# Attention and recurrence of one denoising step, in a fixed order of TensorE

## Chip, cores and metric

The kernel runs on one core of a Trainium2 chip. The metric is the device time of one execution in microseconds (us); smaller is better. Weights and inputs lie in HBM in float32, and so do the outputs.

## What is computed

Two layers of a hybrid network run over 1152 tokens: 1024 latent tokens and 128 context tokens. Each layer projects its input once, gives the columns to three groups of heads, projects their outputs back, and ends with a SwiGLU feed-forward part. The change touches two of the three groups. Cut to that, the reference is:

```python
def _mla_attend(q_nope, q_rope, k_nope, k_rope, v):          # 8 heads, 96 score rows, 64 value columns
    ...
        s = jnp.einsum('bqhd,bkhd->bhqk', qn_i, k_nope) + jnp.einsum('bqhr,bkr->bhqk', qr_i, k_rope)
        prob = jax.nn.softmax(s.astype(F32) * MLA_SCALE, axis=-1).astype(v.dtype)
        return jnp.einsum('bhqk,bkhd->bqhd', prob, v)
...
    def step(S, inp):                                        # RWKV-7: 2 directions, 4 heads of 64
        r_t, w_t, k_t, v_t, kk_t, a_t = inp
        s_kk = jnp.einsum('dbhvk,dbhk->dbhv', S, -kk_t)
        S = S * w_t[..., None, :] + s_kk[..., :, None] * (kk_t * a_t)[..., None, :] + v_t[..., :, None] * k_t[..., None, :]
        return S, jnp.einsum('dbhvk,dbhk->dbhv', S, r_t)
...
    y = out[0] + out[1][:, ::-1]
    mu = jnp.mean(y, -1, keepdims=True)
    var = jnp.mean(jnp.square(y - mu), -1, keepdims=True)
    y = ((y - mu) * lax.rsqrt(var + RW_GN_EPS)).reshape(B, T, RW_W) * p['rw_gn_g'] + p['rw_gn_b']
```

## The kernel before

Nearly all time goes to products of float32 operands. A precise product takes three TensorE instructions (`mm3`, L119 to L121): each operand is split into a high and a low part, and high x high, high x low and low x high are summed in PSUM. Products named f32 in the recurrence are float32 matmuls, which the profile counts as two instructions each.

A layer has a stage in which **attention** (`mla`) and the **recurrence** (`rwkv`) run together. In layer 0 it lies at 369 to 996 us of the profile, in layer 1 at 2319 to 2986 us. Before it stand projections, after it the output projection `w_out` and the feed-forward part.

*Attention.* A unit is one head and 512 latent queries; every second unit also takes the 128 context queries. There are 16 units a layer. For each of a unit's 9 key blocks of 128, `attend` issues a score triple (L119 to L121, 512 columns), an Exp on ScalarE (L767, tile `P`), and two value products (L772), and GpSimd sums the P tiles into `acc` (L774). The softmax needs row maxima: they are found two units ahead by coarse scores (L733, reduced by VectorE at L738 and L744), turned by an identity (`eye`, L751) into row 96 of the query tile `qT`. `load` clears that row by a GpSimd memset (L726) and loads the other 96 from `qd` in DRAM. `mla` is a generator; it yields after three key blocks.

*Recurrence.* The tokens go in 9 segments of 128 (one of context, eight latent), each of 2 chunks of 64, all heads and both directions at once. For a segment `rw_prep` makes the chunk matrices M1 (L965: a tile of 64 rows, upper half first, then lower half, one PSUM bank each) and the transposes BT (L972). `rw_solve` inverts 16x16 diagonal blocks, 14 rows on VectorE (L999, L1000), with the blocks going out to DRAM and back (`ltd`, `Db`, `xbd`, `xz`). `rw_double` (L1022 to L1041) grows the inverses to 64x64. `rw_scan` takes the chunks in order: R, then UV (L1065), then the change of the state UV x BT (L1071) and the outputs, UV x M1 (L1075) and state x AR (L1077), eight of each. `rw_post` (L1119 to L1145) does the group norm, with ScalarE's Sqrt and VectorE's reciprocal (L1129), the bonus and the gate. `rwkv` prepares segments three ahead and calls `next(other)` between these parts to let attention go on.

*What sets the order.* The program is written in that order, but a scheduler sorts each engine's instructions by its own estimates of when operands are ready. On TensorE it interleaves instruction by instruction what stands near in the program. `streams` gives each kind of work its PSUM banks: scores "012", value products "3", prep and post "4", doubling "5", scan "67".

TensorE can be used as one tile of 128x128 or as smaller ones. Scores are 128*128, value products 128*64, L965 and L972 64*128, L1071 and L1075 128*64 in the profile's naming, L1077 and L1065 64*64, the doubling 64*64 and 32*32. Below, a **group** is a run of consecutive matmuls of one tile shape in TensorE's order, a **change** the step from one group to the next.

## Time and profile before

| | |
|---|---|
| runs | 3965.17, 3952.76, 3957.21 us |
| median | 3957.21 us |
| span of the profiled execution | 3970.9 us |
| TensorE busy in it | 3842.4 us (97%) |
| VectorE / ScalarE / GpSimd busy | 2006.7 / 1096.0 / 1311.2 us |
| stage of layer 0 / layer 1 | 627 / 667 us |
| the rest | 2677 us |

The profiled execution is one run of its own; its span is all of its time that the profile gives. PE is TensorE's matmuls, DVE VectorE, ACT ScalarE, POOL GpSimd, SP the engine that issues most DMAs. PEclk is the clock that TensorE was granted, as a share of full speed. Instructions overlap on TensorE, and the ends of matmuls are modelled: what a group costs is read from the start of its first instruction to the start of the next group's, not from busy time.

### The profile page before, as it was taken

The page shows a single profiled execution, that of the slowest core. Times are in us where ns is not written, and L with a number is a line of the kernel's source. Part 1 is how long each engine was busy: PE and PEld are TensorE (multiplying, and loading weights), DVE is VectorE, ACT ScalarE, POOL GpSimd, SP SyncE. Part 2 cuts the span into 40 slices and gives each one's busy share as a digit, 9 for nine tenths or more (in the row PEclk, how much of TensorE's full clock was granted, in tenths as well). Part 3 has the DMA queues.
Part 4 walks back from the last instruction along what each step waited for, and adds up shares of the span by engine and source line. Part 5 has one row for each costly group of instructions (what it writes and reads, how often), then busy time and mean ns, then how long its engine had stood idle before and what let it go on. Part 6 is the DMA issues. An engine that isn't in the chain of part 4 may idle for free. (4 is left out here: it accounts for less than half of the span.)

```text
span 3970.9 us, 61645 instructions
## 1 busy us (share of the span) xinstructions
PE 3842.4 (97%) x25091; PEld 3178.9 (80%) x25091; DVE 2006.7 (51%) x3428; ACT 1096.0 (28%) x2066; POOL 1311.2 (33%) x1221
## 2 busy tenths in 40 slices
PE   8999999998999999999999989999998999999996
PEld 6887666665988888988888966666658999999995
DVE  3556776645643333343555557644457633333346
ACT  3452333234321111111244423321343321111111
POOL 2324544335411111112541445432354311111145
PEclk9998899998999999999999978886899999999998
DMA  7476443213332222122336554331223211111122
GB/s 284 152 225 159 108 98 86 57 48 115 111 118 91 75 85 78 61 64 75 102 122 181 155 126 111 75 83 33 61 91 126 96 43 43 40 39 40 42 89 76
DMA packets 463452, 383.60 MB, mean 97 GB/s; under 512 B 171020, under 2 KB 397192, under 8 KB 461952
## 3 DMA queue, kind: packets, MB, share of 16 engines
q1 hardware_dynamic: 388864, 271.67, 24.7%
q10 hardware_dynamic: 68480, 92.34, 7.0%
q0 software_dynamic: 5824, 15.66, 1.3%
q8 instruction: 197, 3.23, 0.3%
q14 instruction: 87, 0.71, 0.1%
HBM read 277.74 MB, written 101.84 MB: 96 GB/s over the span
## 5 line engine op out<-in xcount | busy, mean ns | idle before, releaser
L121 PE MATMUL b<-hyh,w 128*128 128x384 f32 x2544 | 858.0, 337 | 0.0
L119 PE MATMUL b<-hyh,w 128*128 128x384 f32 x2448 | 822.4, 336 | 0.0
L120 PE MATMUL b<-hyl,w 128*128 128x384 f32 x2448 | 821.3, 335 | 0.0
L316 POOL TENSOR_TENSOR w<-wr,w 128x2048 fp32r<-128x2048 f32 x64 | 297.1, 4642 | 1190.4 <-ACT w L313 987.6
L121 PEld LDWEIGHTS b<-hyh,w 128*128 128x128 f32 x2544 | 478.7, 188 | 24.5 <-issue 23.9
L119 PEld LDWEIGHTS b<-hyh,w 128*128 128x128 f32 x2448 | 459.6, 188 | 20.8 <-issue 19.4
L120 PEld LDWEIGHTS b<-hyl,w 128*128 128x128 f32 x2448 | 459.5, 188 | 9.7 <-issue 8.3
L774 POOL TENSOR_TENSOR acc<-acc,P 128x512 f32<-128x512 f32 x256 | 338.9, 1324 | 375.5 <-ACT P L767 349.6
L1274 DVE TENSOR_TENSOR fs<-fs,b 128x384 f32<-128x384 f32 x132 | 72.9, 553 | 631.2 <-PE b L121 625.6
L313 ACT CAST w<-wr 128x2048 fp32r<-128x2048 f32 (+2 forms) x86 | 161.2, 1874 | 580.7 <-PE b L120 516.4
L120 PE MATMUL b<-w,hidh 128*128 128x512 f32 x756 | 299.5, 396 | 0.0
L121 PE MATMUL b<-w,hidl 128*128 128x512 f32 x756 | 299.4, 396 | 0.0
L119 PE MATMUL b<-w,hidh 128*128 128x512 f32 x756 | 298.3, 396 | 0.0
L126 DVE TENSOR_TENSOR hidl<-fs,hidh 128x384 fp32r<-128x384 f32 x126 | 233.0, 1851 | 81.3 <-ACT hidh L125 79.2
L1288 DVE TENSOR_TENSOR acc<-acc,b 128x512 f32<-128x512 f32 x288 | 191.4, 684 | 139.0 <-PE b L121 139.0
L767 ACT ACTIVATE P<-b 128x512 f32<-128x512 f32 x256 | 148.8, 595 | 363.4 <-PE b L121 324.9
L738 DVE TENSOR_REDUCE mx<-b 128x1 f32<-128x512 f32 x256 | 172.1, 682 | 135.8 <-PE b L733 134.4
L772 PE MATMUL b<-P,vt 128*64 128x256 f32 x1024 | 192.7, 447 | 14.0 <-ACT P L767 13.8
L119 PE MATMUL b<-w,hyh 128*128 128x256 f32 x576 | 167.3, 292 | 9.9 <-issue 3.2
L125 ACT CAST hidh<-fs 128x384 fp32r<-128x384 f32 x126 | 64.4, 512 | 397.3 <-DVE fs L1274 397.3
L119 PEld LDWEIGHTS b<-w,hidh 128*128 128x128 f32 x756 | 142.1, 188 | 35.1 <-issue 1.7
L121 PEld LDWEIGHTS b<-w,hidl 128*128 128x128 f32 x756 | 142.1, 188 | 34.3
(433 smaller groups left out, 7481.0 us busy)
## 6 DMA issues: line engine op xcount, KB each, us to landing
wr<-in_ffn_w_in_dram SPq DMA_DIRECT2D x88, 512.0 KB, 4.7
fx<-in_ada_w_dram SPq DMA_DIRECT2D x28, 1024.0 KB, 5.1
wr<-in_ffn_w_out_dram SPq DMA_DIRECT2D x22, 1024.0 KB, 4.9
wr<-in_ada_w_dram SPq DMA_DIRECT2D x20, 1024.0 KB, 9.1
zin<-zd SPq DMA_DIRECT2D x36, 384.0 KB, 4.2
xres<-x ACTq DMA_DIRECT2D x27, 512.0 KB, 3.6
wr<-in_w_in_dram SPq DMA_DIRECT2D x12, 1024.0 KB, 6.1
qT<-qd SPq DMA_DIRECT2D x32, 384.0 KB, 6.4
```

The lines of the kernel that those rows point to most:

```text
L119: mm(out, ah, bh, start=(i == 0), stop=False)
L120: mm(out, ah, bl, start=False, stop=False)
L121: mm(out, al, bh, start=False, stop=(i == n - 1))
L126: (lo_eng or self.nc.vector).tensor_tensor(lo, src, hi.bitcast(F32), op=ALU.subtract)
L313: self.nc.scalar.copy(hi, r)
L316: (eng or self.nc.gpsimd).tensor_tensor(lo[:, s], r[:, s], hi[:, s].bitcast(F32), op=ALU.subtract)
L738: nc.vector.tensor_reduce(mx[:, i, c:c + 1], p, axis=AX.X, op=ALU.max)
L767: nc.scalar.activation(P[:, 0:nq], p[:, 0:nq], AF.Exp, scale=MLA_SCALE)
L772: nc.tensor.matmul(po[64 * i:64 * i + 64, 0:w], vt[:, kt_], P[:, w * i:w * i + w], start=(n == 0), stop=(kt_ == kts[-1]))
L774: nc.gpsimd.tensor_tensor(acc[:, 0:nq], acc[:, 0:nq], P[:, 0:nq], op=ALU.add)
L1274: nc.vector.tensor_tensor(s, s, u[:, 0:BLK], op=ALU.mult)
L1288: nc.vector.tensor_tensor(acc[i][:, w], acc[i][:, w], p, op=ALU.add)
```

## The change

Only the stage changes; the code outside it stays as it is.

*Attention* goes in batches of key blocks: [0,1], [2,3], [4,5], [6,7], [9], the context's block with the last. A batch issues its score triples and one or two steps for the maxima of the unit two ahead; its value products are issued one batch later (`before`). The generator yields twice a batch: behind the scores and behind the value products. Row 96 of `qT` comes with the load from `qd`, which got a row of zeros in `fill`.

*Recurrence* goes in slots. A slot lets attention issue a batch's scores, does its `first` work, three rows of a running solve, lets attention issue value products, and does its other work. `rw_prep`, `rw_solve`, `rw_double`, `rw_scan` and `rw_post` became generators that yield behind whole groups of matmuls. There are 69 slots a layer: 10 ahead of the first scan, 6 for each of 9 segments, 5 behind. `RW_PACE` gives attention an extra batch now and then. Segments are prepared two ahead.

*Order.* From `mla` to the end of attention TensorE's instructions stay in the order of the program (`manual_schedule`); the other engines are sorted as before.

*Groups.* `rw_prep` alternates between the two halves of rows, with a PSUM bank for each. `rw_scan` issues all of UV x BT, then all of UV x M1, then all of state x AR, into one bank. `rw_post` takes the root of four numbers a token on GpSimd, and two matmuls by the identity spread them.

Attention and its helper steps:

```diff
+RW_PACE = 1.08
...
+        self.qd = d([8, 97, 2, T], "qd")
...
+        for h in range(8):
+            nc.scalar.dma_start(self.qd[h, 96].rearrange("x t -> (x t)").rearrange("(p n) -> p n", p=128), o[:, 0:18])
...
-            nc.gpsimd.memset(t[96:97, 0].bitcast(F32), 0.0)
-            nc.sync.dma_start(t[0:96].bitcast(F32), self.qd[h, :, :, q0:q0 + nq])
+            nc.sync.dma_start(t[0:97].bitcast(F32), self.qd[h, :, :, q0:q0 + nq])
...
-        def attend(h, q0, kT, vt, qT, steps, slots):
...
+        def scores(kT, qT, kt_, nq, P):
+            ks = slice(128 * kt_, 128 * kt_ + 128)
+            p = self.psum("as")
+            self.mm3(p[:, 0:nq], [(kT[0][:, ks], kT[1][:, ks], qT[0], qT[1])])
+            nc.scalar.activation(P[:, 0:nq], p[:, 0:nq], AF.Exp, scale=MLA_SCALE)
+        def finish(h, q0, nq, po, acc):
...
-                P = self.t(ap, [128, 512], "P", bufs=3) if n else acc
-                p = self.psum("as")
...
-                slots[0] -= 1
-                for _ in range(-(-len(steps) // (slots[0] + 1))):
-                    steps.pop(0)()
-                for i in parts:
-                    nc.tensor.matmul(po[64 * i:64 * i + 64, 0:w], vt[:, kt_], P[:, w * i:w * i + w], start=(n == 0), stop=(kt_ == kts[-1]))
...
-                if n % 3 == 2 and n < 8:
-                    yield
...
-            yield
+            steps = [carry, *prepare(n + 2)[1:]]
...
+            for g, kts in enumerate(([0, 1], [2, 3], [4, 5], [6, 7], [9])):
+                todo = steps[g] if g < len(steps) else []
+                for k in kts:
+                    P = Ps[k] = self.t(ap, [128, 512], "P", bufs=4)
+                    scores(kT, qT, k, 512, P)
+                    if k:
+                        nc.gpsimd.tensor_tensor(acc, Ps[0] if k == 1 else acc, P, op=ALU.add)
...
+                yield
+                if before:
+                    before()
+                def products(h=h, q0=q0, vt=vt, acc=acc, po=po, Ps=Ps, kts=kts, ctx=ctx):
+                    if not po:
+                        po.append(self.psum("po"))
+                    for k in kts:
+                        for i in range(2):
+                            nc.tensor.matmul(po[0][64 * i:64 * i + 64, 0:256], vt[:, k], Ps[k][:, 256 * i:256 * i + 256], start=(k == 0), stop=(k == 9))
...
+                before = products
...
+                yield
+            carry = steps[5] if len(steps) > 5 else []
```

The slots of `rwkv`:

```diff
+        def solved(i):
+            while i in solves:
+                row()
+        pace = [0.0]
+        def slot(*work, first=()):
+            pace[0] += RW_PACE - 1
+            if pace[0] >= 1:
+                pace[0] -= 1
+                next(other, None)
-        for n in range(len(segs) + ahead):
-            if n < len(segs):
-                ready[n] = self.rw_prep(segs[n], rp, hv)
-                attend(2 if n < ahead else 1)
-                xz[n] = self.rw_solve(rp, ready[n][3], self.xbd[n % 4])
-            i = n - ahead
...
-            if i >= 0:
-                self.rw_double(rp, ready[i][3], xz[i], Q)
...
+            next(other, None)
+            for f, *a in first:
+                f(*a)
+            for _ in range(3):
+                row()
+            next(other, None)
+            for f, *a in work:
+                f(*a)
...
+        next(other)
+        start(0)
+        slot((go, prep, 0))
+        slot((go, prep, 0), (solve, 0), (start, 1))
+        slot((go, prep, 0))
+        slot((go, prep, 1))
+        slot((go, prep, 1), (solve, 1))
+        slot((go, prep, 1))
+        slot((solved, 0), (go, double, 0))
+        for _ in range(3):
+            slot((go, double, 0))
+        for i in range(n):
+            scan = self.rw_scan(segs[i], rp, Y, state, xz[i], *ready[i])
+            j = i + 2
+            def turn():
+                next(scan, None)
...
+            def posting():
+                for p in posts:
+                    next(p, None)
+            slot((turn,), (start, j))
+            slot((turn,), (go, prep, j), first=[(posting,)])
+            slot((turn,), (go, prep, j), (solve, j), first=[(solved, i + 1), (go, double, i + 1), (posting,)])
+            slot((turn,), (go, prep, j), first=[(go, double, i + 1), (posting,)])
+            slot((turn,), first=[(go, double, i + 1), (posting,)])
+            slot((turn,), first=[(go, double, i + 1), (posting,)])
...
+            ready.pop(i), xz.pop(i)
+        posts = [self.rw_post(l, b, rp, Y, g2, brk) for b in post]
+        for _ in range(5):
+            slot(*((next, p, None) for p in posts))
```

`rw_prep`, `rw_solve` and `rw_double`:

```diff
+        M1 = self.t(rp, [128, 2, 4, 2, 128], "M1", bufs=3)
+        BT = self.t(rp, [128, 2, 4, 2, 64], "BT", bufs=3)
...
+        yield AR, EP, UV, M1, BT
...
-        for h in range(2):
-            for j in range(2):
-                p = self.psum("ra").rearrange("p (c t) -> p c t", t=128)
-                for ct in range(2):
-                    for u in range(2):
-                        nc.tensor.matmul(p[:, 2 * ct + u], BK[u][rows[h], 2 * j + ct, bks[h]], AR[u][rows[h], 2 * j + ct], start=True, stop=True)
...
+                    for h in range(2):
+                        nc.tensor.matmul(ps[h][:, 2 * ct + u], BK[u][rows[h], 2 * j + ct, bks[h]], AR[u][rows[h], 2 * j + ct], start=True, stop=True)
...
+            yield
+        ps = [self.psum("ra") for _ in range(2)]
+        for cj in range(4):
+            for u in range(2):
+                for h in range(2):
-                    nc.tensor.transpose(p[:, o:o + 64], BK[u][rows[h], cj, bks[h]], self.ident[rows[h], rows[h]])
-            nc.scalar.copy(BT[:, h].rearrange("p c u k -> p (c u k)"), p)
-        return AR, EP, UV, M1, BT
+                    nc.tensor.transpose(ps[h][:, o:o + 64], BK[u][rows[h], cj, bks[h]], self.ident[rows[h], rows[h]])
...
-        return xz
+        yield xz
...
-            return self.psum("rb")[:, 0:256].rearrange("p (j b t) -> p j b t", b=2, t=16)
+            return self.psum("ra")[:, 0:256].rearrange("p (j b t) -> p j b t", b=2, t=16)
```

`rw_scan`, `rw_post` and `run`:

```diff
+            p = self.psum("rc")
+            ps_, po = (p[:, a:a + 256].rearrange("p (c u t) -> p c u t", c=2, u=2) for a in (0, 256))
...
-                cj = 2 * j + ct
-                nc.tensor.matmul(po[rg, ct, u], UV[:, h, u, cj, :], M1[:, h, cj, u, 64:128], start=True, stop=(S is None))
-                if S is not None:
-                    nc.tensor.matmul(po[rg, ct, u], S[rg, ct, u, :], AR[u][rg, cj, 64:128], start=False, stop=True)
+                nc.tensor.matmul(ps_[rg, ct, u], BT[:, h, 2 * j + ct, u, :], UV[:, h, u, 2 * j + ct, :], start=True, stop=True, skip_group_check=True)
+            for n, (h, ct, u, rg) in enumerate(gu):
+                nc.tensor.matmul(po[rg, ct, u], UV[:, h, u, 2 * j + ct, :], M1[:, h, 2 * j + ct, u, 64:128], start=(n < 2 or S is None), stop=(S is None), skip_group_check=True)
+            if S is not None:
+                for h, ct, u, rg in gu:
+                    nc.tensor.matmul(po[rg, ct, u], S[rg, ct, u, :], AR[u][rg, 2 * j + ct, 64:128], start=False, stop=True, skip_group_check=True)
...
-    def rw_post(self, l, blocks, rp, Y, g2, brk):
...
+    def rw_post(self, l, b, rp, Y, g2, brk):
...
+        yield
+        p = self.psum("ra")
+        for ct in range(2):
+            nc.tensor.matmul(p[:, 2 * ct:2 * ct + 2], sq[:, ct], self.bones[:, 0:128:64], start=True, stop=True)
+        q = self.t(rp, [128, 4], "po_q", bufs=2)
+        nc.vector.tensor_scalar(q, p[:, 0:4], 1.0 / 64, 64e-5, op0=ALU.mult, op1=ALU.add)
+        self.rsqrt(q, q, 4)
+        wide = tmp("po_t")
+        nc.gpsimd.tensor_copy(wide.rearrange("p c (h o) -> p (c h) o", o=64), q.rearrange("p (c o) -> p c o", o=1).to_broadcast([128, 4, 64]))
...
-        nc.tensor.matmul(p, self.bones, sq, start=True, stop=True)
-        s = tmp("po_t")
-        nc.vector.tensor_scalar(s, p, 1.0 / 64, 64e-5, op0=ALU.mult, op1=ALU.add)
-        nc.scalar.activation(s, s, AF.Sqrt)
-        nc.vector.reciprocal(s, s)
-        nc.gpsimd.tensor_tensor(yc, yc, s, op=ALU.mult)
...
+            nc.tensor.matmul(p[:, ct], wide[:, ct], self.ident, start=True, stop=True)
+        nc.vector.tensor_tensor(yc, yc, p, op=ALU.mult)
...
-            self.streams(**{"as": "012", "po": "3", "ra": "4", "rb": "5", "rc": "67"})
+            self.streams(**{"as": "0127", "po": "3", "ra": "45", "rc": "6"})
...
+            order = ExitStack()
+            order.enter_context(self.tc.manual_schedule(engines={mybir.EngineType.PE}))
...
+            order.close()
```

The order of TensorE shows what this does. In the names, `b` is a PSUM bank, `xz` the inverses, `S` the state, the numbers tell tiles apart; line numbers of the changed kernel are its own (scores L120 to L122, coarse scores L736, `eye` L754, value products L861, L1061 for L965, L1070 for L972, L1178, L1181 and L1184 for L1071, L1075 and L1077).

TensorE at the outputs of a chunk, layer 0, before (`M` is M1, `UV` and `S` as above):

```order
L1071 MATMUL b_1347_7284<-UV_5125,BT_5127 64x64
L1075 MATMUL b_1348_7293<-M_912_5126,UV_5125 64x64
L1077 MATMUL b_1348_7293<-AR_919_5144,S_6786 64x64
L1075 MATMUL b_1348_7293<-M_912_5126,UV_5125 64x64
L1077 MATMUL b_1348_7293<-AR_919_5144,S_6786 64x64
L1075 MATMUL b_1348_7293<-M_912_5126,UV_5125 64x64
L1077 MATMUL b_1348_7293<-AR_927_5171,S_6786 64x64
L1075 MATMUL b_1348_7293<-M_912_5126,UV_5125 64x64
L1077 MATMUL b_1348_7293<-AR_927_5171,S_6786 64x64
L1075 MATMUL b_1348_7293<-M_912_5126,UV_5125 64x64
L1077 MATMUL b_1348_7293<-AR_919_5144,S_6786 64x64
L772 MATMUL b_1331_7207<-P_7222,vt_6383 64x256 x2
```

TensorE at the same place in the changed kernel:

```order
L1178 MATMUL b_1089_6141<-UV_4496,BT_4498 64x64 x8
L1181 MATMUL b_1089_6141<-M_758_4497,UV_4496 64x64 x8
L1184 MATMUL b_1089_6141<-AR_765_4515,S_5874 64x64 x2
L1184 MATMUL b_1089_6141<-AR_773_4542,S_5874 64x64 x2
L1184 MATMUL b_1089_6141<-AR_765_4515,S_5874 64x64 x2
L1184 MATMUL b_1089_6141<-AR_773_4542,S_5874 64x64 x2
L120 MATMUL b_1096_6179<-qT_550_3683,kT_556_3689 128x512
L121 MATMUL b_1096_6179<-qT_550_3683,kT_556_3689 128x512
L122 MATMUL b_1096_6179<-qT_550_3683,kT_556_3689 128x512
```

Eight products of UV and M1 now stand together, and then eight of the state, where the two alternated one by one.

TensorE at scores among the doubling of the recurrence, layer 0, before:

```order
L972 MATMUL b_1286_6959<-cst_63,BK_1279_6915 128x64
L1022 MATMUL b_1421_7620<-xz_5902,M_1028_5705 64x32 x5
L119 MATMUL b_1337_7223<-qT_578_3777,kT_581_3780 128x512
L120 MATMUL b_1337_7223<-qT_578_3777,kT_581_3780 128x512
L121 MATMUL b_1337_7223<-qT_578_3777,kT_581_3780 128x512
L1022 MATMUL b_1421_7620<-xz_5902,M_1028_5705 64x32 x6
L772 MATMUL b_1331_7207<-acc_7208,vt_6383 64x256 x2
L1071 MATMUL b_1347_7284<-UV_5125,BT_5127 64x64 x7
L733 MATMUL b_1334_7214<-kT_582_3781,qT_577_3776 128x512
L733 MATMUL b_1335_7217<-kT_582_3781,qT_577_3776 128x512
```

The same place of TensorE in the changed kernel:

```order
L120 MATMUL b_1066_6017<-qT_552_3685,kT_555_3688 128x512
L121 MATMUL b_1066_6017<-qT_552_3685,kT_555_3688 128x512
L122 MATMUL b_1066_6017<-qT_552_3685,kT_555_3688 128x512
L736 MATMUL b_1067_6023<-kT_556_3689,qT_551_3684 128x512
L120 MATMUL b_1069_6027<-qT_552_3685,kT_555_3688 128x512
L121 MATMUL b_1069_6027<-qT_552_3685,kT_555_3688 128x512
L122 MATMUL b_1069_6027<-qT_552_3685,kT_555_3688 128x512
L736 MATMUL b_1070_6033<-kT_556_3689,qT_551_3684 128x512
L754 MATMUL b_1071_6036<-eye_3679 97x128
L1136 MATMUL b_1072_6039<-xz_5741,M_873_5069 32x32 x16
L861 MATMUL b_1040_5844<-P_5892,vt_4442 64x256 x2
L861 MATMUL b_1040_5844<-P_5902,vt_4442 64x256 x2
```

A score triple stood alone between pieces of the doubling; now two triples with their coarse scores stand together, and the doubling and the value products of the batch before follow as wholes.

TensorE at the transposes in `rw_prep`, layer 0, before, all in one bank (BK's half of rows is the same in all eight):

```order
L1022 MATMUL b_1421_7620<-xz_5902,M_1028_5705 64x32
L972 MATMUL b_1286_6959<-cst_63,BK_1271_6888 128x64
L972 MATMUL b_1286_6959<-cst_63,BK_1279_6915 128x64
L972 MATMUL b_1286_6959<-cst_63,BK_1271_6888 128x64
L972 MATMUL b_1286_6959<-cst_63,BK_1279_6915 128x64
L972 MATMUL b_1286_6959<-cst_63,BK_1271_6888 128x64
```

The same place of TensorE in the changed kernel:

```order
L1163 MATMUL b_1061_5977<-S_5874,AR_773_4542 64x64
L1070 MATMUL b_1063_5996<-cst_63,BK_1002_5677 128x64
L1070 MATMUL b_1064_5997<-cst_63,BK_1002_5677 128x64
L1070 MATMUL b_1063_5996<-cst_63,BK_1010_5704 128x64
L1070 MATMUL b_1064_5997<-cst_63,BK_1010_5704 128x64
L1070 MATMUL b_1063_5996<-cst_63,BK_1002_5677 128x64
```

Neighbours now lie in different banks and in different halves of the rows.

## Rows read from the trace of the kernel before

**Rows 1.** Page, the span in 40 slices, tenths: VectorE and the clock granted.

```profile
DVE  3556776645643333343555557644457633333346
PEclk9998899998999999999999978886899999999998
```

**Rows 2.** Windows: length, busy time (instructions) of each engine, clock, DMA share, GB/s.

```profile
369.00:996.00 627.00, 601.38 (x5241) 400.13 (x5242) 397.11 (x788) 211.84 (x425) 282.95 (x333) 0.90 0.37 90
2319.00:2986.00 667.00, 644.79 (x5202) 422.41 (x5201) 386.77 (x777) 209.31 (x419) 275.04 (x319) 0.83 0.33 80
500.00:900.00 400.00, 395.50 (x3979) 266.49 (x3979) 246.43 (x507) 127.06 (x258) 160.33 (x186) 0.95 0.32 72
```

**Rows 3.** Timeline of TensorE, layer 0: start, length, engine, line, operation, tile.

```profile
554.93 0.68 PE L1065 MATMUL b<-R,xz 64*64 64x64 f32 x16
555.55 0.65 PE L772 MATMUL b<-P,vt 128*64 128x256 f32 x4
556.13 0.50 PE L733 MATMUL b<-kT,qT 128*128 128x512 f32 x1
...
932.70 1.08 PE L772 MATMUL b<-P,vt 128*64 128x256 f32 x8
933.71 0.50 PE L119 MATMUL b<-qT,kT 128*128 128x512 f32 x1
```

**Rows 4.** The same timeline, score triples and row halves of the preparation.

```profile
424.77 1.16 PE L965 MATMUL b<-AR,BK 64*128 64x128 f32 x8
425.86 0.50 PE L119 MATMUL b<-qT,kT 128*128 128x512 f32 x1
...
427.45 0.44 PE L772 MATMUL b<-P,vt 128*64 128x256 f32 x2
...
611.87 0.50 PE L119 MATMUL b<-qT,kT 128*128 128x512 f32 x1
...
612.76 0.24 PE L1028 MATMUL b<-xz,Q 64*64 64x32 f32 x1
```

**Rows 5.** The same timeline, outputs of a chunk.

```profile
614.16 0.69 PE L1071 MATMUL b<-UV,BT 128*64 128x64 f32 x16
614.67 0.28 PE L1075 MATMUL b<-M,UV 128*64 128x64 f32 x2
...
615.39 0.33 PE L1077 MATMUL b<-AR,S 64*64 64x64 f32 x2
```

**Rows 6.** Timeline of TensorE, layer 1, transposes of the preparation.

```profile
2502.85 0.71 PE L972 MATMUL b<-cst,BK 64*128 64x64 f32 x8
2503.49 0.30 PE L751 MATMUL b<-eye 128*97 128x128 f32 x1
```

**Rows 7.** Groups of VectorE, 369 to 996 us: count, busy, mean ns, idle before, releaser.

```profile
L738 DVE TENSOR_REDUCE mx<-b 128x1 f32<-128x512 f32 x128 | 85.8, 683 | 54.2 <-PE b L733 53.4
L999 DVE TENSOR_TENSOR pr_x<-Xb,Db 64x4 f32<-64x4 f32 (+6 forms) x126 | 68.4, 543 | 2.6
...
L1000 DVE TENSOR_REDUCE Xb<-pr_x 64x2 f32<-64x4 f32 (+6 forms) x126 | 29.2, 232 | 2.5
...
L126 DVE TENSOR_TENSOR hyl<-wr,hyh 128x384 fp32r<-128x384 f32 (+1 forms) x23 | 17.1, 799 | 4.8 <-ACT hyh L125 4.8
L1129 DVE RECIPROCAL po_t<-po_t 128x256 f32<-128x256 f32 x9 | 15.7, 1748 | 4.7 <-ACT po_t L1128 4.7
```

**Rows 8.** DMA issues of the program: count, KB each, median us to landing.

```profile
xz<-xbd SPq DMA_DIRECT2D x72, 128.0 KB, 3.2
...
ltd<-M SPq DMA_DIRECT2D x36, 128.0 KB, 2.6
...
xbd<-Xb SPq DMA_DIRECT2D x36, 64.0 KB, 2.6
...
Db<-ltd SPq DMA_DIRECT2D x18, 64.0 KB, 2.6
```

**Rows 9.** Windows as in Rows 2, two stretches of like work in the two layers.

```profile
700.00:762.00 62.00, 62.00 (x607) 40.85 (x607) 38.13 (x89) 14.13 (x31) 22.44 (x25) 0.92 0.17 36
2700.00:2763.00 63.00, 63.00 (x374) 41.27 (x372) 21.22 (x51) 9.61 (x21) 12.80 (x17) 0.51 0.15 31
```

More of the change, by code (lines that the diff above doesn't have):

```diff
@@ new lines, in rwkv, with start, go, solve @@
+        ready, xz, prep, double, post = {}, {}, {}, {}, []
+        def start(i):
+            if i < n:
+                prep[i] = self.rw_prep(segs[i], rp, hv)
+                ready[i] = next(prep[i])
+        def go(stream, i):
+            if i in stream:
+                next(stream[i], None)
+        solves = {}
+        def solve(i):
+            if i < n:
+                solves[i] = self.rw_solve(rp, ready[i][3], self.xbd[i % 4])
+        def row():
+            for i in sorted(solves):
+                x = next(solves[i])
+                if x is not None:
+                    xz[i] = x
+                    double[i] = self.rw_double(rp, ready[i][3], x, Q)
+                    del solves[i]
+                return
@@ new lines, in rw_post @@
+        for ct in range(2):
+            nc.vector.tensor_scalar(yc[:, ct], yc[:, ct], self.v(l, "rw_gn_g", ct), self.v(l, "rw_gn_b", ct), op0=ALU.mult, op1=ALU.add)
+        yield
+        p = bank()
+        for ct in range(2):
+            for d in range(2):
+                nc.tensor.matmul(p[:, ct], brk[:, ct], rk[:, 2 * d + ct], start=(d == 0), stop=(d == 1))
+        q = tmp("po_t")
+        nc.vector.tensor_tensor(q, p, vg[:, 0:2], op=ALU.mult)
+        nc.gpsimd.tensor_tensor(yc, yc, q, op=ALU.add)
```

168 lines of the change are left out of this document (79 added, 89 removed).

## Prediction, made before the result was known

> **What bounds the kernel now.** I read the page first. TensorE works in 97% of the span, and no other engine comes near; only in the two stages with attention and recurrence does the granted clock fall to 0.7 and 0.8, while VectorE stands at 5 to 7 tenths there [rows 1]. The busy time by windows then puts the two stages apart [rows 2]. They last 627 and 667 us, 1294 together, and TensorE is busy for all but 25.6 and 22.2 us of them. So the stage is bound by TensorE, not by waits. But not all of its time is work: the granted clock is 0.90 and 0.83 on the mean. The time given to the low clock is 627 x 0.10 + 667 x 0.17 = 63 + 113 = 176 us, so at full speed the same order would take 1294 - 176 = **1118 us**. Like work shows it: 62 us at a clock of 0.92 hold 607 matmuls, 63 us at 0.51, the lower of the two levels (1.2 of 2.4 GHz) in nearly all of it, hold 374, both with TensorE busy throughout [rows 9].
>
> The timeline says what those 1118 us hold. A run of matmuls of one tile shape costs more than its members: there is a price for the change. Four value instructions last 0.58 us to the next group, eight 1.01 [rows 3]; four more cost 0.43, so the change costs 0.58 - 0.43 = 0.15. Six scores last 1.59 us, three alone 0.89 [rows 4]; three inside a group cost 0.70, so the change is 0.19. In the outputs of a chunk, UV x M1 and state x AR alternate in shape, one matmul each: three steps take 0.72 us, 0.24 each, where eight matmuls in one group take 0.51 [rows 5]. With 0.19 for its change, that is 0.04 for a matmul, and 0.24 - 0.04 = 0.20 for each change. These prices, 0.15 to 0.20 us, count in full on the engine that sets the end.
>
> **The change part by part.**
>
> *Fewer changes of shape.* In TensorE's order I count the groups of one shape in the two stages: 945 and 964 before, 306 and 304 changed. That removes 1299. At 0.19 us, the price in the middle of the scores, it is 1299 x 0.19 = **-247 us**; the ends are 195 (0.15) and 260 (0.20). Of it 34 chunks with a state give 14 changes each, 476 in all; the rest is scores, value products and doubling that now stand in whole groups. These are seconds of TensorE, with no other work beneath.
>
> *Halves of rows.* `rw_prep` issues 288 chunk matmuls (L965) and 288 transposes (L972). Four of the first, all in one half, take 1.09 us [rows 4], less a change 0.90, 0.225 each, so 65 us; eight of the second take 0.64 [rows 6], less a change 0.45, 0.056 each, so 16 us; 81 together. Would two halves run at the same time? Eight UV matmuls (L1065), 16 instructions, go to two diagonal 64*64 tiles in turn: 0.62 - 0.19 = 0.43 us [rows 3], 0.027 for an instruction of 64 columns where the transposes pay 0.056. That is half the price for work that alternates between halves. No row shows it for 64*128 tiles, so the ends are 0 and -40, half of 81; I take **-25 us**, nearer to the halving.
>
> The Trainium skill, page "TensorEngine Tiling (Array Packing)", section Key Properties, says that different tiles can load weights and multiply in parallel. By that rule the halves would give the whole 40 us, and the sum below would end some 16 us lower; no run here shows it for this tile.
>
> *Waits that a fixed order adds.* Before, the scheduler fills a gap of TensorE with what is ready. Now, if a score waits for a PSUM bank, the recurrence behind it in TensorE's queue waits too. The stage has 69 slots a layer, with two hand-overs each to attention: 138 slots of both layers. The nearest row for such a wait is a row maximum, 0.683 us [rows 7], after which a bank of the four comes free. One for each slot is 138 x 0.683 = 94 us; none is the lower end, two the upper (188). I take one: two triples and two coarse scores of one batch fill all four banks, so the first bank of the next batch comes free only behind an Exp or a row maximum. At the two ends of both stages nothing from outside may fill in any more; a round trip of 2.6 + 2.6 us over DRAM [rows 8] at each of four ends is 21 us. Together **+115 us** (21 to 209).
>
> *What is off the path.* The memset of row 96 and the load with one row more, eight small DMAs at the start, the group norm without VectorE's 1.75 us reciprocal [rows 7] and without Sqrt on ScalarE, the multiply that goes from GpSimd to VectorE, and two small matmuls for each block: these lie on engines that are idle for a third of the stage or more [rows 2], so I cost them at nothing; the cover is TensorE's own work. If VectorE became the bound, the reciprocal would be worth 2 x 15.7 = 31 us. Three buffers in place of four for M1, BT and xz match the preparation two ahead in place of three.
>
> *The sum.* 1118 - 247 - 25 + 115 = 961 us at full clock. Which clock? Where the stage before is steady, from 500 to 900 us, it is 0.95 [rows 2], and with fewer and longer groups I see no reason for less: 961 / 0.95 = 1012 us. The stages shrink by 1294 - 1012 = 282, and the profiled execution goes from 3970.9 to 3689. That profile stands 13.7 us above the median of the runs, so the forecast is **3675 us**.
>
> **The rivals.**
>
> *VectorE becomes the bound.* Its work in the stages is 397 + 387 = 784 us [rows 2]; 31 go with the reciprocal, and some 34 with output-projection splits that now come behind the stage (17.1 in layer 0 [rows 7], about as much in layer 1, an estimate). With TensorE faster, 719 us must fit. For it speaks that a solve is a chain on one engine, 14 rows of two dependent instructions, and that row maxima wait in the same queue. If VectorE can't be denser than its 246.43 of 400 us [rows 2], 0.616, the stages need 719 / 0.616 = 1167 us: 3970.9 - 1294 + 1167 - 13.7 = 3830. Against it: slices with 7 tenths exist [rows 1].
>
> *The clock stays low.* If short waits at 138 slots keep the clock where it is on the mean, (0.90 + 0.83) / 2 = 0.865, the stages take 961 / 0.865 = 1111 us and the time is 3774. For it: layer 1 had whole stretches at 0.51 with TensorE busy throughout [rows 9], so busy time alone doesn't keep it up.
>
> The Trainium skill speaks for this rival: "TensorE: Matmul & The Clock Gate", section "A second HAM failure mode: psum-queue depth-cycling", tells of a kernel whose short idle times between groups, as it went round its PSUM banks, let the clock go up and down. The rows before show low clock in work without idle time, so they neither bear it out nor exclude it.
>
> *Slower: the inverses stand in the fixed order.* Slot 3 of a segment first drains the solve of the next (`solved`), and TensorE then stands at the first matmul of `rw_double` until its inverses have come back. The chain is 2.6 + 2.6 + 14 x (0.543 + 0.232) + 2.6 + 3.2 = 21.9 us [rows 7, 8]. If all of it were bare in each of 18 segments it would cost 394: the stages take 1012 + 394 = 1406 and the time is 4069. It decides from 282 / 18 = 15.7 us a segment. Against it: the solve starts six slots earlier, and at 1012 / 138 = 7.3 us a slot it has 44 us for 22.
>
> *The change of shape is free on the path*, its price only the way in which this trace models ends: then nothing of 247 comes, waits of about that size eat the rest, and the time stays 3957.
>
> *Better than forecast.* If waits are only the 21 us at the ends and the clock is 0.98, as it mostly is outside the stages [rows 1], the stages take (846 + 21) / 0.98 = 885 us and the time is 3548.
>
> **How the numbers follow.** Chances: forecast 0.70, VectorE 0.10, low clock 0.10, better 0.05, slower 0.03, free 0.02. The forecast's own ends: no change of the clock but two maxima a slot, 1055 / 0.95 = 1111, give 3774; the price at 0.15 gives 52 / 0.95 = 55 more, 3730; both together would be 3829. At the other end, 60 us of waits with a clock of 0.98, 906 / 0.98 = 924, give 3587. The range 3590 to 3800 leaves out VectorE, slower, free and better, 0.20 together. About 0.3% (12 us) is what a measurement can tell from no change: faster by more in all cases but the free one (same, 0.02) and the slower one (0.03), so 0.95.
>
> **What would show it.** In the profile after: stages of some 480 to 530 us each; a granted clock of 0.93 or more in them; the outputs of a chunk in three runs of about 0.5 us each; two score triples with coarse scores in one run; idle time of TensorE in the stages of 100 to 170 us in place of 48, ended by row maxima. Alternating halves show as a group of eight L1061 matmuls in 1.5 us or less, where one after the other they would take 8 x 0.225 + 0.19 = 2.0. It is wrong if the idle time passes 250 us, if TensorE waits at the first doubling matmul of a segment for the inverses, or if the clock is below 0.87.

## The result, and the profile after

The changed kernel is slower: 4262.44 us (4259.4 to 4265.02) against 3961.19 us before (four runs, the three of the table above and one more), a ratio of 1.0778 with a 95% interval of 1.0741 to 1.0816. The forecast was 3675 us, and the range ended at 3800.

| profiled execution | before | after |
|---|---|---|
| span | 3970.9 us | 4257.6 us |
| stage of layer 0, from the first coarse score to the last product of attention | 626.5 us | 760.6 us |
| stage of layer 1 | 665.6 us | 704.7 us |
| idle TensorE in the two stages | 47.8 us | 501.0 us |
| the rest | 2678.8 us | 2792.3 us |

From the page of the changed kernel, the span in 40 slices: TensorE, the clock granted, and the DMA engines' share.

```profile
PE   8994565668799999999999956756578899999997
...
PEclk9997677778899999999999977778788999999998
DMA  8463422322333232121335533232124211111122
```

In the stages TensorE is now at 4 to 8 tenths, where it was full or nearly so:

```profile
PE   8999999998999999999999989999998999999996
```

The same in numbers, by windows of the two stages (length, busy time of each engine, clock, DMA share, GB/s), which answers [rows 2]:

```profile
389.00:1149.60 760.60, 487.96 (x5207) 356.48 (x5207) 359.88 (x767) 180.07 (x388) 274.41 (x315) 0.76 0.28 70
2546.00:3250.70 704.70, 476.34 (x5172) 348.64 (x5171) 351.21 (x761) 171.66 (x377) 266.87 (x298) 0.79 0.27 68
```

TensorE's busy time fell by 282 us, from 1246 to 964. But it stood idle for 501 us, and the clock went down to 0.76 and 0.79. So the question is who makes it wait. The groups of TensorE in the stage of layer 0, and then of layer 1, with the idle time ahead of them and what ended it:

```profile
L736 PE MATMUL b<-kT,qT 128*128 128x512 f32 (+1 forms) x192 | 73.7, 452 | 180.0 <-DVE mx L741 51.1 <-DMA qT<-qd 49.3 <-DMA kT<-kd 40.9
```

```profile
L736 PE MATMUL b<-kT,qT 128*128 128x512 f32 (+1 forms) x192 | 73.7, 452 | 127.8 <-DMA qT<-qd 50.6 <-DMA kT<-kd 40.9 <-ACT P L763 14.4
```

308 us of the 501 stand ahead of one line: the coarse scores of the unit two ahead, which need the query tile `qT` and the keys `kT`. The timeline of SyncE's queue shows two of these loads; columns are start, time the issue took, line and tile:

```profile
622.09 0.66 SPq L730 DMA_DIRECT2D qT<-qd  x1
622.85 8.95 SPq L789 DMA_DIRECT2D kT<-kd  x1
...
678.37 0.67 SPq L730 DMA_DIRECT2D qT<-qd  x1
```

and the timeline of TensorE behind the second one:

```profile
684.95 0.40 PE L122 MATMUL b<-qT,kT 128*128 128x512 f32 x1
696.78 0.77 PE L736 MATMUL b<-kT,qT 128*128 128x512 f32 x1 [11.44 <-DMA qT<-qd]
```

Issued at 678.37, used at 696.78: the load took 18.4 us. Before, it landed in 6.4 us on the median (count, KB each, median us to landing):

```profile
qT<-qd SPq DMA_DIRECT2D x32, 384.0 KB, 6.4
```

What the DMA engines did meanwhile is in a window of the changed kernel between the two:

```profile
680.00:694.00 14.00, 5.35 (x51) 3.59 (x49) 2.37 (x5) 3.01 (x6) 3.25 (x3) 0.82 0.07 25
```

and, for comparison, a window behind a load of the query tile in the kernel before:

```profile
648.50:653.00 4.50, 4.50 (x49) 3.33 (x50) 4.34 (x12) 1.98 (x5) 4.28 (x5) 1.00 0.61 178
```

A mean share of 0.07 of 16 engines is about one engine, at 25 GB/s; before, 0.61 of them moved 178 GB/s. The packets say the same: for 12.9 of these 14 us exactly one of them was under way. At 25 GB/s, 388 KB take 16 us. What changed in this transfer is its number of rows, 97 in place of 96; the 97th is read from DRAM, where the memset wrote it before. The load also holds up the queue: the issue of the keys right behind it took 8.95 us here, and 8.4 to 9.2 us in all ten places where the keys follow a query tile, so the keys are late as well. In the run with 96 rows below, the same issue takes 0.48 to 0.56 us in its ten places.

The Trainium skill has this rule, on the page "DMA: Bandwidth & Descriptors", section "Why a DMA increments its semaphore by 16 and not by 1": a copy goes to the largest number of engines up to 16 that divides the slowest dimension of both sides. 96 gives 16; 97 is a prime and gives one. The trace agrees, with 0.07 of 16 engines at work. I had not weighed this rule.

### The profile page after: what moved, and what is told of

The parts are those of the page before. It is cut to its first block, busy times and chain, and to the rows that moved or that the text cites. A ratio compares the mean times of both kernels' runs of the same rounds, so it can differ in the third digit from the quotient of the medians.

```text
span 4257.6 us, 61765 instructions
## 1 busy us (share of the span) xinstructions
PE 3597.6 (84%) x25199; PEld 3091.9 (73%) x25199; DVE 1960.1 (46%) x3428; ACT 1040.9 (24%) x2012; POOL 1299.4 (31%) x1191
## 4 chain that ended last, share of the span: by engine, by line
PE 53%; DMA 12%; DVE 7%; issue 3%; POOL 2%; SPq 2%; ACT 1%; ACTq 0%; POOLq 0%; DVEq 0%
PE b L120 15%; PE b L122 14%; PE b L121 14%; DMA qT<-qd 3%; PE b L861 2%; DMA kT<-kd 2%; DMA xbd<-Xb 1%; PE b L243 1%; SPq L730 1%; PE b L356 1%; DVE hyl L127 1%; DMA szin<-sd 1%; PE b L736 1%; DVE pr_x L1097 1%; DMA wr<-in_w_out_dram 1%
## 5 line engine op out<-in xcount | busy, mean ns | idle before, releaser
L122 PE MATMUL b<-hyh,w 128*128 128x384 f32 x2544 | 858.0, 337 | 0.0
L120 PE MATMUL b<-hyh,w 128*128 128x384 f32 x2448 | 822.4, 336 | 0.0
L122 PEld LDWEIGHTS b<-hyh,w 128*128 128x128 f32 x2544 | 478.7, 188 | 24.8 <-issue 23.9
L120 PEld LDWEIGHTS b<-hyh,w 128*128 128x128 f32 x2448 | 459.7, 188 | 20.8 <-issue 19.4
L736 PE MATMUL b<-kT,qT 128*128 128x512 f32 (+1 forms) x384 | 147.4, 452 | 307.8 <-DMA qT<-qd 99.9
L841 POOL TENSOR_TENSOR acc<-acc,P 128x512 f32<-128x512 f32 x224 | 295.7, 1320 | 361.3 <-ACT P L763 356.1
L736 PEld LDWEIGHTS b<-kT,qT 128*128 128x128 f32 x384 | 81.1, 232 | 349.5 <-issue 189.8
L122 PE MATMUL b<-w,hidl 128*128 128x512 f32 x756 | 299.4, 396 | 0.0
L120 PE MATMUL b<-w,hidh 128*128 128x512 f32 x756 | 298.3, 396 | 0.0
L763 ACT ACTIVATE P<-b 128x512 f32<-128x512 f32 x288 | 169.8, 596 | 438.3 <-PE b L122 365.2
L861 PE MATMUL b<-P,vt 128*64 128x256 f32 x1152 | 189.1, 452 | 0.3 <-ACT P L763 0.3
L120 PE MATMUL b<-w,hyh 128*128 128x256 f32 x576 | 171.9, 300 | 20.1 <-ACT w L317 13.2
L121 PE MATMUL b<-w,hyh 128*128 128x256 f32 x576 | 170.6, 297 | 3.3 <-DVE w L320 3.3
```

The costliest lines, as they stand in the source:

```text
L120: mm(out, ah, bh, start=(i == 0), stop=False)
L121: mm(out, ah, bl, start=False, stop=False)
L122: mm(out, al, bh, start=False, stop=(i == n - 1))
L736: nc.tensor.matmul(p[:, 0:n], qT[0][:, 128 * i:128 * i + 128], kT[0][:, k0:k0 + n], start=True, stop=True)
L763: nc.scalar.activation(P[:, 0:nq], p[:, 0:nq], AF.Exp, scale=MLA_SCALE)
L841: nc.gpsimd.tensor_tensor(acc, Ps[0] if k == 1 else acc, P, op=ALU.add)
```

## The experiments

Theory A is that transfer. Rival B is that the fixed order puts the first use too near to the issue, whatever the load takes. Ratios are to the kernel before, measured beside each run.

**The load of 96 rows again.**

```diff
-            nc.sync.dma_start(t[0:97].bitcast(F32), self.qd[h, :, :, q0:q0 + nq])
+            nc.gpsimd.memset(t[96:97, 0].bitcast(F32), 0.0)
+            nc.sync.dma_start(t[0:96].bitcast(F32), self.qd[h, 0:96, :, q0:q0 + nq])
```

> The changed kernel, but the query tile is loaded with 96 rows again and row 96 is cleared by GpSimd as before; all else of the change stays. Theory A (the transfer): in the trace of the changed kernel the DMA traffic stands at about 25 GB/s for some 16 us behind every load of a query tile of 388 KB, and TensorE waits at the first coarse score of each unit for it; a load of 96 rows landed in 6.4 us before. Then these waits nearly go (about 180 us in layer 0, as much in layer 1), the clock comes back to 0.92 or more in the stages, and the time is 3680 to 3760 us. Rival B (the distance): a load is issued only when the unit before is through, two batches ahead of its first use, which the fixed order makes too late whatever the load takes; then most of the wait stays and the time is 4050 us or more.

Measured: 3815.97 us (3809.88 to 3819.79), ratio 0.9665 (0.9615 to 0.9715). One line of 446 us turns the change from a loss into a gain. DMA issues by line with count, size and median us to landing, and TensorE's wait at the coarse scores in layer 0 (L737 here):

```profile
qT<-qd SPq DMA_DIRECT2D x32, 384.0 KB, 4.4
kT<-kd SPq DMA_DIRECT2D x16, 640.0 KB, 7.2
```

```profile
L737 PE MATMUL b<-kT,qT 128*128 128x512 f32 (+1 forms) x192 | 65.8, 412 | 17.2 <-DVE rc L779 10.5 <-DVE mx L742 4.2 <-ACT P L764 1.1
```

180.0 us became 17.2, and hardly any of it is for a load. Rival B falls: when the load lands in 4.4 us, the same distance suffices. The clock came back less far than theory A said, to 0.90, and the time is 56 us over its upper end; that is taken up below.

**The same load in the kernel before**, its only edit (with the row of zeros in `qd`):

```diff
-            nc.gpsimd.memset(t[96:97, 0].bitcast(F32), 0.0)
-            nc.sync.dma_start(t[0:96].bitcast(F32), self.qd[h, :, :, q0:q0 + nq])
+            nc.sync.dma_start(t[0:97].bitcast(F32), self.qd[h, :, :, q0:q0 + nq])
```

> The kernel before with the one edit of the load: 97 rows from DRAM in place of 96 rows and a GpSimd memset. Theory A: its query loads too run at about 25 GB/s for 16 us; there the scheduler's order leaves some 30 us between the issue and the next unit's need, so part of it is hidden, and it costs 20 to 150 us: 3980 to 4110. Rival B: a load of 97 rows is as good as one of 96, and the time stays within 0.3% of before.

Measured: 4419.19 us (4400.81 to 4437.44), ratio 1.1202 (1.1121 to 1.1282). The edit alone costs 465 us, three times the upper end of what I expected. So the loss does not need the fixed order: the scheduler's order does not hide the load either, and why not, no run shows. The coarse scores in layer 0 (L734 here), and the windows of both stages:

```profile
L734 PE MATMUL b<-kT,qT 128*128 128x512 f32 (+1 forms) x192 | 86.9, 516 | 165.9 <-DMA qT<-qd 139.7 <-ACT qTc L753 16.3 <-DVE eye L745 8.6
```

```profile
388.70:1244.20 855.50, 662.84 (x5246) 436.68 (x5248) 393.80 (x786) 212.60 (x425) 274.07 (x307) 0.76 0.25 65
2605.80:3422.40 816.60, 673.70 (x5184) 438.96 (x5184) 386.81 (x779) 208.73 (x418) 266.10 (x300) 0.75 0.26 66
```

The waits are 193 and 143 us. Of the 438 us between the two profiled executions 288 are such waits; 90 are busy time that grew for the same work, with the clock at 0.76 and 0.75 in place of 0.90 and 0.83 [rows 2]; and 58 lie outside the stages.

**97 rows in two DMAs, 96 and 1.**

```diff
-            nc.sync.dma_start(t[0:97].bitcast(F32), self.qd[h, :, :, q0:q0 + nq])
+            nc.sync.dma_start(t[0:96].bitcast(F32), self.qd[h, 0:96, :, q0:q0 + nq])
+            nc.sync.dma_start(t[96:97].bitcast(F32), self.qd[h, 96:97, :, q0:q0 + nq])
```

> The changed kernel with the load of 97 rows split into two DMAs, one of 96 rows and one of the row of zeros; no memset. Theory A: the large one lands like that of 96 rows before, and the time is within 0.7% of the kernel that clears the row by GpSimd (3680 to 3780 us). Rival B: no better than the changed kernel, 4200 us or more. A third possibility, that the row of 97 costs by its number of bytes in DRAM and not by its number of rows, would also leave it slow.

Measured: 3842.29 us (3836.09 to 3850.04), ratio 0.9734 (0.9682 to 0.9786); 0.7% over the kernel with the memset, as theory A has it; that both are over its figures in us is the same shortfall. The row from DRAM is not at fault.

**112 rows.**

```diff
-        self.qd = d([8, 97, 2, T], "qd")
+        self.qd = d([8, 112, 2, T], "qd")
...
-            nc.sync.dma_start(t[0:97].bitcast(F32), self.qd[h, :, :, q0:q0 + nq])
+            nc.sync.dma_start(t[0:112].bitcast(F32), self.qd[h, :, :, q0:q0 + nq])
```

> The changed kernel, no memset, with the query tile loaded with 112 rows in place of 97 (qd gets 16 rows of zeros): 448 KB in place of 388. If the slow load of 97 rows comes from its count of rows (97 is a prime; 96 and 112 are multiples of 16), this one is as good as 96 rows: 3800 to 3850 us, landing in 5 to 8 us. If it comes from the bytes, from the row that lies in another place, or from the zeros being written by the ScalarE queue, it stays slow: 4250 us or more.

Measured: 3823.83 us (3818.9 to 3833.26), ratio 0.9697 (0.963 to 0.9763), and the issue's line:

```profile
qT<-qd SPq DMA_DIRECT2D x32, 448.0 KB, 4.4
```

15 rows and 60 KB more, and it lands in 4.4 us. So it is the count of rows, not the bytes, not the zeros, not the missing memset. That the memset is gone gains nothing either (3824 us against 3816 with it). Together these four settle the main cause. Other counts that are no multiple of 16 were not run.

**Alternating outputs**, on the kernel with 96 rows:

```diff
             for n, (h, ct, u, rg) in enumerate(gu):
                 nc.tensor.matmul(po[rg, ct, u], UV[:, h, u, 2 * j + ct, :], M1[:, h, 2 * j + ct, u, 64:128], start=(n < 2 or S is None), stop=(S is None), skip_group_check=True)
-            if S is not None:
-                for h, ct, u, rg in gu:
+                if S is not None:
                     nc.tensor.matmul(po[rg, ct, u], S[rg, ct, u, :], AR[u][rg, 2 * j + ct, 64:128], start=False, stop=True, skip_group_check=True)
```

> The kernel with 96 rows and GpSimd's memset, but the outputs of a chunk alternate again, one product of UV and M1 and one of the state by turns, as before the change; nothing else moves. If a change of tile shape costs TensorE 0.20 us on the path, 34 chunks with 14 changes more cost 476 x 0.20 = 95 us at full clock, about 100 us with the clock of the stage: slower than the kernel with 96 rows by 80 to 120 us. Rival: the price is only how the trace models the ends of matmuls, or the stage is now bound by waits that hide it; then the two agree within 0.5%.

Measured: 3926.62 us (3911.95 to 3939.53), ratio 0.9957 (0.9921 to 0.9994), 111 us over the kernel with 96 rows. The price of a change is real and on the path. The windows of the two stages show what the 111 us are:

```profile
389.50:986.30 596.80, 528.41 (x5208) 391.44 (x5207) 358.81 (x767) 178.74 (x386) 284.49 (x333) 0.85 0.35 85
2340.80:2916.80 576.00, 513.54 (x5171) 380.14 (x5171) 353.49 (x760) 172.09 (x377) 274.77 (x317) 0.87 0.35 82
```

The traces count 476 more groups. With each busy moment of TensorE weighted by the clock granted in it, its work in the stages is 900 us at full speed in place of 814: 86 us more, 0.18 for each change. Its idle time is less, 131 us in place of 168, and the clock is lower, 0.85 and 0.87 in place of 0.90. The 0.23 us that 111 / 476 gives is the sum of these three, not the price of one change.

**The same grouping alone, in the kernel before**: eight products of UV and M1, then eight of the state, nothing else.

> The kernel before with one edit: the outputs of a chunk in two groups, eight products of UV and M1, then eight of the state. In the order 34 chunks lose most of their 14 changes of shape each. At 0.20 us, with the scheduler breaking a few groups by other work, 350 to 476 changes go: 70 to 95 us at full clock, 75 to 110 with the clock of the stage, so 3850 to 3885 against 3957. Rival: in the order of before other waits take the place; then 3940 to 3960.

Measured: 3874.69 us (3850.89 to 3883.1), ratio 0.9774 (0.9711 to 0.9838). 79 us from one loop written in another way. The scheduler left most groups whole: 738 and 755 groups of one shape in the stages in place of 934 and 946, counted in the traces by the tile shapes that the profile names. TensorE's work at full speed, weighted as above, fell from 1073 to 1002 us, 0.18 for each of the 387 changes. Its idle time rose from 48 to 85 us, and the clock from 0.90 and 0.83 to 0.91 and 0.94, so this gain, too, is a sum of three.

**Halves of rows one after the other**, on the kernel with 96 rows:

```diff
-            for ct in range(2):
-                for u in range(2):
-                    for h in range(2):
+            for h in range(2):
+                for ct in range(2):
+                    for u in range(2):
                         nc.tensor.matmul(ps[h][:, 2 * ct + u], BK[u][rows[h], 2 * j + ct, bks[h]], AR[u][rows[h], 2 * j + ct], start=True, stop=True)
```

and the same for the transposes.

> The kernel with 96 rows and a memset, with rw_prep's matmuls and transposes one half of the rows after the other again (each half still in its own bank). In the trace of the changed kernel eight L1061 matmuls take 1.09 us, as long as four of one half took before, and 16 transposes 0.64, as long as eight. So the halves run at the same time, and undoing it costs 36 groups of 1.09 - 0.19 and 18 of 0.64 - 0.19, 32 + 8 = 40 us at full clock, 35 to 50 us over the kernel with 96 rows (3816). Rival: the halves only fill time in which TensorE would wait anyway; then within 12 us.

Measured: 3845.4 us (3840.82 to 3851.87), ratio 0.975 (0.9684 to 0.9816), 29 us over the kernel with 96 rows. The timeline of TensorE in this kernel, and then in the changed one, at one group of eight such matmuls:

```profile
500.81 1.71 PE L1062 MATMUL b<-AR,BK 64*128 64x128 f32 x16
502.45 0.50 PE L120 MATMUL b<-qT,kT 128*128 128x512 f32 x1
```

```profile
620.00 1.16 PE L1061 MATMUL b<-AR,BK 64*128 64x128 f32 x16
621.09 0.50 PE L120 MATMUL b<-qT,kT 128*128 128x512 f32 x1
```

1.64 us against 1.09: 36 groups x 0.55 = 20 us, and the 18 groups of transposes take 0.95 against 0.64. My expectation priced the other side as twice the 0.90 us of four matmuls of one half [rows 4], which with a change is 2.0 us. Four of one half and then four of the other, in one group, took 1.64, so part of the gain is there already without alternating.

**No fixed order**, on the kernel with 96 rows: the line with `manual_schedule` goes, the program stays in batches and slots.

> The kernel with 96 rows and a memset, but TensorE's instructions in the stage are sorted by the scheduler again; the program is written in batches and slots as changed. Theory: the gain comes from whole groups, which only the fixed order keeps; then groups break up and much of the 140 us goes back: 3880 to 3980 us. Rival: the way the program is written is enough and the fixed order only adds waits (168 us of idle TensorE in the stages); then it is faster than 3816, down to 3740.

Measured: 3796.83 us (3790.18 to 3806.15), ratio 0.9627 (0.956 to 0.9694), 19 us under the kernel with 96 rows, whose runs lay from 3810 to 3820. My theory falls. The windows of its two stages:

```profile
369.90:908.90 539.00, 494.15 (x5188) 346.30 (x5188) 352.09 (x770) 177.10 (x387) 286.80 (x341) 0.91 0.42 100
2259.50:2783.80 524.30, 483.91 (x5180) 341.62 (x5178) 356.74 (x763) 170.98 (x379) 277.27 (x327) 0.93 0.39 91
```

Inside the stages the traces show an even trade: groups of one shape rise from 335 and 333 to 535 and 512, idle TensorE falls from 91.3 and 77.1 us to 44.8 and 40.4, and the two stages take 1063.3 us against 1065.9. So of the 1212 groups that went between the kernel before and the one with 96 rows, the way the program is written accounts for 833 and the fixed order for 379; what the fixed order saves in changes it pays in waits. The gain lies outside the stages, which are 17 us shorter there. In the kernel with 96 rows TensorE waits ahead of both stages for the load of the latent state, whose transposes (L902) stand first in the fixed order:

```profile
387.35 0.34 PE L902 MATMUL b<-cst,so 64*128 64x64 f32 x1 [20.95 <-DMA UV<-vtd]
```

```profile
2285.84 0.34 PE L902 MATMUL b<-cst,so 64*128 64x64 f32 x1 [9.21 <-DMA so<-in_state_rwkv_dram]
```

In layer 0 the view names another load that landed late; the transpose behind it waits 0.80 us more for `so`, the state itself. Without the fixed order other work stands ahead of these transposes, and TensorE waits 1.7 us in all for that load.

**The latent state's transposes later**, on the kernel with 112 rows: they move from the head of `rwkv` to just ahead of the scans.

> The kernel with 112 rows, with the transposes of the first latent state (L902, which stand first in the fixed order and wait 21 us in layer 0 for their load) moved to just ahead of the scans. If TensorE then begins with attention at once, 10 to 20 us come back in layer 0, and 0 to 5 in layer 1: 12 to 25 us under the kernel with 112 rows. If the coarse scores wait for their own loads as long, nothing changes.

Measured: 3802.38 us (3800.29 to 3813.94), ratio 0.9638 (0.9559 to 0.9716), 21 us under the kernel with 112 rows: what stands first in a fixed order and waits for a load, everything behind it waits for too. It is within the spread of the kernel without a fixed order (3797 us), so with this one move no cost of the fixed order is left that these runs can tell.

**No extra batches** (RW_PACE 1.0), without a fixed order:

> The kernel with 96 rows without a fixed order, with RW_PACE at 1.0 in place of 1.08: no extra batches of attention, so more of attention is left when the recurrence ends. The leftover is dense work of TensorE, so little should move: within 0.5% of 3797. Rival: the recurrence alone is too thin at the batches' pace and attention alone waits for its maxima at the end: 10 to 30 us slower.

Measured: 3792.0 us (3784.01 to 3806.28), ratio 0.958 (0.9511 to 0.9649): nothing moved that can be told.

**The group norm of before**, without a fixed order: one matmul of the squares with `bones`, Sqrt, reciprocal and GpSimd's multiply, in the changed kernel's steps.

> The kernel with 96 rows without a fixed order, with the group norm of before (Sqrt on ScalarE with its table loads, VectorE's reciprocal of 128x256, multiply on GpSimd) in the changed kernel's steps. The prediction costed the new norm at nothing, since VectorE has 35% and ScalarE 65% of the stage free: within 0.4% of 3797. Rival: table loads (2 x 1.28 us each time) stand in front of an Exp that the value products wait for, 18 blocks: 10 to 45 us slower.

Measured: 3765.72 us (3762.74 to 3766.26), ratio 0.9507 (0.9454 to 0.956), 31 us under the same kernel with the new norm (26 under the one with RW_PACE 1.0), and the fastest of all here. Neither side had expected a gain. TensorE's groups of the norm over both stages, new (L1242 and L1233) and then old (L1232):

```profile
L1242 PE MATMUL b<-cst,po_t 128*128 128x128 f32 x72 | 13.0, 299 | 0.0
...
L1233 PE MATMUL b<-cst,po_t 128*128 128x2 f32 x72 | 11.3, 262 | 0.0
```

```profile
L1232 PE MATMUL b<-po_t,cst 128*128 128x256 f32 x36 | 11.7, 416 | 0.0
```

The new norm takes work from VectorE and ScalarE, which have time, and gives TensorE, which has none, 24.3 us of busy time where the old one gave it 11.7. In the profiled executions the two stages are 20 us shorter with the old norm and the rest 18. The windows of the stages with the old norm:

```profile
369.30:899.90 530.60, 486.36 (x5157) 338.35 (x5157) 371.38 (x772) 195.60 (x409) 285.83 (x332) 0.93 0.43 102
2240.30:2753.00 512.70, 474.88 (x5125) 326.17 (x5125) 370.19 (x767) 192.82 (x405) 276.59 (x318) 0.94 0.41 96
```

Idle time is nearly the same (82 us against 85), and so is busy time weighted by the clock granted (906 us in both). What differs is the clock, 0.93 and 0.94 in place of 0.91 and 0.93. So the measured gain is shown, and its cause is not: neither the fewer matmuls nor the longer chain of the new norm (GpSimd's root and copy, one step more) accounts for it in these figures.

## Why the prediction was wrong, step by step

*The step that failed* is an item of "What is off the path": "the load with one row more" was costed at nothing, with TensorE's work as its cover. It cost 446 us. Between the profiled executions it is 440: 333 of waits in the stages (501 against 168 without it); 67 of longer busy time there, with the clock at 0.76 and 0.79 in place of 0.90; and 40 outside the stages. The prediction gives no landing time for this load, before or after; by costing it at nothing it took the old one, 6.4 us, to hold for the new shape. The bound from both sides that I gave to other unseen costs I did not give to this one. The sign I named for being wrong (over 250 us of idle time, a clock under 0.87) did show. The place I named, the inverses at the first doubling matmul, showed only in part: TensorE waits for them 14.7 us in layer 0 and 30.1 in layer 1 of the changed kernel, 45 of the 501, and 19.3 and 14.6 with 96 rows.

*With that one line mended*, the other steps can be held against the kernel with 96 rows (3816 us; forecast 3675, 141 us too low). Windows of its two stages:

```profile
389.00:930.50 541.50, 450.17 (x5208) 335.31 (x5207) 356.03 (x767) 177.70 (x385) 286.16 (x333) 0.90 0.39 93
2287.60:2812.00 524.40, 447.31 (x5172) 331.88 (x5171) 349.88 (x760) 171.55 (x377) 274.06 (x317) 0.90 0.38 90
```

- *Fewer changes of shape*, -247 us at 0.19: the mechanism is right, and its size about right. Two runs give 0.18 us of TensorE's time at full speed for a change, near the 0.19 of the prediction; putting 476 back costs 111 us in time, and doing only these in the kernel before gains 79. The other changes were not measured apart. In the traces 1212 groups go, not the 1299 counted in the order of the program (1880 before, 668 with 96 rows). TensorE's work in the stages at full speed fell from 1073 to 814 us, 259, where changes and halves together were to give 272; some 24 of the 259 only moved out of the stages, as told below. The timeline of the changed kernel shows the three groups that were named, 0.46, 0.57 and 0.61 us from start to start, where sixteen matmuls by turns stood before [rows 5]:

```profile
625.90 0.63 PE L1178 MATMUL b<-UV,BT 128*64 128x64 f32 x16
626.36 0.64 PE L1181 MATMUL b<-M,UV 128*64 128x64 f32 x16
626.93 0.68 PE L1184 MATMUL b<-AR,S 64*64 64x64 f32 x16
627.54 1.16 PE L1061 MATMUL b<-AR,BK 64*128 64x128 f32 x16
```

- *Halves of rows*, -25: the mechanism is right, and the agreement in size partly luck. Undoing the alternation alone costs 29 us in time and 25 in the groups (20 for the matmuls, and 18 x 0.31 = 6 for the transposes). But the prediction's sum starts from the kernel before, 81 us, and by its own prices the alternating groups hold 36 x (1.09 - 0.19) + 18 x (0.64 - 0.19) = 40 us: the whole halving came, the end that I had not taken. The other 15 us are there as soon as both halves stand in one group.
- *Waits*, +115 in all, of it 94 in the stages: idle TensorE is 168.4 us there, 120.6 over before. A little low, and only in part from the place that I had named. An Exp (`P`), the reciprocal of the softmax sums (`rc`) or a row maximum (`mx`), behind which a score bank comes free, ends 56 us of it (27, 22 and 7.5), most of them waits of the coarse scores and of the `eye` matmuls. The largest single releaser is the inverses' way over DRAM, 34 us in both layers, which I had taken only as a rival.
- *The ends of the stages*, +21: this was mis-sized. The rest of the kernel grew from 2678.8 to 2752.1, by 73 us. The traces count 148 output-projection matmuls that before filled gaps inside the stages (119 and 67) and now stand behind them (37 and 1 are left inside), and TensorE's busy time outside the stages grew by 24 us (2598 to 2623). Its idle time there grew by 49 (81 to 129); 32 of it is the wait at the latent state's transposes, 21.8 in layer 0 and 10.1 in layer 1.
- *The clock*, 0.95 by the steady part of the stage before: it is 0.90, between that and the rival of 0.865. 0.90 x 1066 = 959 us at full clock, where my sum had 961; the agreement is partly luck, since the 24 us that left the stage are not in my sum. At 0.95 the stages would take 1010 us, so this term is 56 us of the 141.
- *The group norm* was costed at nothing as well. It cost 31 us, though on the kernel without a fixed order, and by what way stays open.

As measured, the span of that kernel is 3970.9 - 1292.1 + 1065.9 + 73.3 = 3818.0, where the prediction had 3689 for it: 54 us more in the stages, all by the clock, and 75 outside them. None of the rivals with a chance named the cause; the one for a slower kernel came nearest, with a DMA that stands bare on the path, but it named the wrong transfer and the fixed order as the reason, and the kernel before loses 465 us by the same load without a fixed order.

What stays open: why the clock is 0.90 with 168 us of idle time and 0.91 and 0.93 with 85, but was 0.90 and 0.83 in the kernel before with 48. Idle time alone does not order these.

## What to carry to other kernels

Before a load that changes shape is costed by the old landing time, look at its number of rows: here 97 rows in place of 96 left it about one of sixteen DMA engines. An edit that "comes with" a large change deserves a run of its own; here the batches, the groups and the row halves were worth 140 us and more, and one line outside them lost 446. And group matmuls of one tile shape in the program's text first: doing that in one loop alone gave 79 us, while fixing the order by hand on top of it was even in the stages, and lost time where the first thing in it waited for a load.

## What the runs showed that I had not expected

- A load of 97 rows kept about one of 16 DMA engines busy: 0.07 of their time, 25 GB/s, 18.4 us; 96 and 112 rows land in 4.4.
- Such a load holds its queue: the next issue on SyncE, the keys', took 8.4 to 9.2 us in ten places of ten, where it took 0.48 to 0.56 right behind a load of 96 rows.
- A change of tile shape costs TensorE 0.15 to 0.20 us at full clock by the groups, 0.18 by two runs that move 476 and 387 of them.
- Eight matmuls on 64*128 tiles that alternate between the two halves of rows take 1.09 us, as long as four of one half alone [rows 4]; four of one half and then four of the other take 1.64.
